# Taking the second block of the first group into the V product unnormalised, and normalising both blocks afterwards

## The chip, the cores and the metric

One core of one Trainium2 chip. The metric is the device time of one execution in microseconds (us). TensorE multiplies matrices and writes its results to PSUM; VectorE and ScalarE do the elementwise work; GpSimd stores most results to HBM and takes reciprocal square roots; SyncE issues the loads.

## The reference, cut to what matters

One encoder layer on x of 2048 positions by 1024 channels:

```python
h = rms_norm(x, norm_g[l])                      # x * rsqrt(mean(x*x)) * g, by position
proj = jnp.einsum("bsd,de->bse", h, w_in[l])    # 6 parts of 1024 columns
a_val, a_gate, g_conv, u, v, g_sgu = jnp.split(proj, split_points, axis=-1)
y_conv = conformer_conv_branch(a_val, a_gate, ...) * silu(g_conv)
y_sgu = (u * (w_s @ layer_norm(v) + b_s)) * silu(g_sgu)   # w_s: 128x128 by head, in chunks of 128 positions
x = x + jnp.einsum("bse,ed->bsd", jnp.concatenate([y_conv, y_sgu], -1), w_out[l])
return rms_norm(x, final_g)
```

The change concerns the first lines: how h is formed for the first 1024 positions, and when it has to exist for the part called v. Because the factor rsqrt(mean(x*x)) belongs to a position, it can be multiplied into h before the product or into a row of v after it.

## The kernel before, in words

Every fp32 operand is split into a high part in fp32r and the remainder (`split`, L127: ScalarE makes the high part, VectorE the low part), and each product is three matrix products: high by high, low by high, high by low. The positions stand in four blocks of 512. A group is two blocks: group 0 is blocks 0 and 1, group 1 is blocks 2 and 3. `group(g, A, vtiles)` runs once for each.

A group begins with V, the 1024 columns of v in two halves. `v_mm(A, b, half, tiles, done, hooks)` (L192) multiplies one block by one half of the columns: 96 matmuls of 128x512, over 8 k-steps, 3 products and 4 chunks of 128 positions, into 4 PSUM tiles. A hook is a call written behind k-step k. So V is four such calls: blocks 0 and 1 with the first half, then both with the second half. `done` takes the four PSUM tiles out: for the first half to `v0t` and on to HBM, for the second half into `z`, whose mean and variance are taken, normalised (L288, ScalarE) and passed chunk by chunk to `mix` (L213): 8 small matmuls into two `mixp` tiles, copied by ScalarE to `mixt` (L220) and stored.

Behind V come 20 units. A unit is seven products of 12 matmuls each (a scheme with seven in place of eight block products), named x, z, y, v and again x and v by their PSUM tiles (L347). The operands are sums of blocks of a (s1 to s4, `sums_of_a`) and of weights (`unit_weights`, L304), whose raw tiles `w` are loaded by SyncE at L311 and L312 into the small pool of three row tiles. The same pool holds the first three chunks' `z`, the raw V weights `vraw` and, ahead of group 1, the raw `xs` of blocks 2 and 3. A depthwise convolution (L464 to L478) fills VectorE at low priority. Towards the end of group 0 the same stream of code makes group 1's h (`staged_h`: VectorE L143, then split into `a`) and splits group 1's V weights (`v_weights`: `vh` on ScalarE, `vl` on VectorE). Group 1's V begins when these are there.

At the very start of group 0, block 0 doesn't wait for its mean square. `X[0]` is x scaled by g alone, split into high and low (`xg`, L544 and L545), and `v0_done_scaled` (L251) multiplies each chunk's rows by the factor `row_rs[0]` as it takes them out of PSUM. Block 1 in before is normalised first: `squares` (L550) gives sums of squares, `stats_of` a factor by position (matmuls `pc`, VectorE `col`, GpSimd `rs`), `rows_of` spreads it over partitions (VectorE `dg`, matmul `rb_x`), and `normalise` multiplies and splits x (VectorE L143, then `a` on ScalarE and VectorE).

The program is written in this order, but a scheduler of the framework decides at build time in which order each engine gets its instructions, by priorities and by a timeline that it simulates; on the chip each engine's order is fixed.

## Time and profile before

| what | us |
|---|---|
| median of 3 runs | 1380.39 (1379.97 to 1381.41) |
| the profiled execution's own time | 1378.5 |
| its span in the trace | 1376.7 |
| TensorE busy in it | 1342.3 |
| VectorE busy in it | 1134.8 |
| ScalarE busy in it | 584.8 |

The span is the profiled execution's first to last instruction; 1.8 us of that execution's own time lie around it, and the median of the runs is another 1.9 us above it. A busy share near the whole span says that an engine had work nearly always, not that each of its instructions ran at its best rate.

### The profile page before, as it was taken

To read this page: it belongs to the slowest core of one execution; us is meant where nothing else is said; L and a number is where in the kernel's file an instruction comes from. 1 tells how busy PE (TensorE), PEld (TensorE's weight loads), DVE (VectorE), ACT (ScalarE), POOL (GpSimd) and SP (SyncE) were. 2 spreads that over 40 slices of the span, in tenths; PEclk is the share of its full clock that TensorE was granted. 3 is DMA by queue.
4 is the path that set the end of the run, shared out by engine and by line. 5 is a ranking of instruction groups with operands and counts; after the bars stand their busy time and mean duration, and the time that the engine had idled before them with its cause. 6 is when DMAs were issued, how large, how long until landed. Compare 5 with 4: busy or idle time off the path is not lost.

```text
span 1376.7 us, 17691 instructions
## 1 busy us (share of the span) xinstructions
PE 1342.3 (97%) x6044; PEld 1108.7 (81%) x6044; DVE 1134.8 (82%) x1787; ACT 584.8 (42%) x987; POOL 198.0 (14%) x378
## 2 busy tenths in 40 slices
PE   7999999999999999999999999999999999999996
PEld 5688888888888878878888888888878888888875
DVE  6975599999899999999899999998998224677763
ACT  5547444443545443353322222221344333656652
POOL 0101323323323310110111011110000000010110
PEclk9999999999999999999999999999999999999998
DMA  6227999898989885369877778777689444555541
GB/s 249 85 88 250 372 345 324 302 315 298 320 300 343 292 301 191 98 236 337 291 252 262 254 261 293 261 262 258 211 262 296 163 152 163 158 175 180 171 147 46
DMA packets 167450, 329.14 MB, mean 239 GB/s; under 512 B 15040, under 2 KB 84672, under 8 KB 167360
## 3 DMA queue, kind: packets, MB, share of 16 engines
q1 hardware_dynamic: 119040, 208.46, 45.9%
q0 software_dynamic: 31424, 111.17, 22.3%
q10 hardware_dynamic: 16896, 8.39, 2.2%
q8 instruction: 47, 0.77, 0.2%
q14 instruction: 43, 0.35, 0.1%
HBM read 191.12 MB, written 136.84 MB: 238 GB/s over the span
## 4 chain that ended last, share of the span: by engine, by line
PE 73%; DVE 11%; issue 9%; DMA 4%; POOL 1%; ACT 1%; SPq 0%; POOLq 0%; DVEq 0%; ACTq 0%
PE x L347 17%; PE pa L703 13%; PE po L703 12%; PE v L347 11%; PE v L198 7%; PE y L347 6%; PE z L347 5%; DVE ca L469 2%; DVE cb L477 2%; PE mixp L218 1%; DVE cb L471 1%; DMA xrow<-in_x_dram 1%; DVE op L130 1%; DMA mix_sp<-mixt 1%; DMA op_sp<-ex 1%
## 5 line engine op out<-in xcount | busy, mean ns | idle before, releaser
L469 DVE SCALAR_TENSOR_TENSOR ca<-cx,cwt,ca 128x505 f32<-128x505 f32 (+1 forms) x240 | 180.5, 752 | 0.0
L471 DVE SCALAR_TENSOR_TENSOR cb<-cx,cwt,cb 128x504 f32<-128x504 f32 (+1 forms) x224 | 168.2, 751 | 6.7 <-ACT cb L465 2.8
L477 DVE SCALAR_TENSOR_TENSOR cb<-cq,cws,cb 128x504 f32<-128x504 f32 (+1 forms) x224 | 167.6, 748 | 0.5
L347 PE MATMUL x<-s,op 128*128 128x512 f32 x624 | 151.6, 390 | 1.4 <-ACT s L129 1.4
L347 PEld LDWEIGHTS x<-s,op 128*128 128x128 f32 x624 | 116.8, 188 | 26.2 <-ACT s L129 1.7
L198 PE MATMUL v<-vh,a 128*128 128x512 f32 x448 | 121.0, 394 | 3.7 <-ACT a L129 3.4
L198 PEld LDWEIGHTS v<-vh,a 128*128 128x128 f32 x448 | 84.2, 189 | 23.2 <-ACT a L129 4.2
L347 PE MATMUL z<-s,op 128*128 128x512 f32 x336 | 82.2, 391 | 0.7 <-DVE s L130 0.5
L347 PE MATMUL x<-s,ex 128*128 128x512 f32 x336 | 81.4, 390 | 0.0
L347 PE MATMUL x<-a,op 128*128 128x512 f32 x312 | 79.1, 391 | 0.0
L347 PE MATMUL y<-a,op 128*128 128x512 f32 x312 | 76.1, 391 | 0.8 <-DMA op<-op_sp 0.8
L347 PE MATMUL v<-s,op 128*128 128x512 f32 x312 | 75.3, 390 | 0.0
L347 PE MATMUL v<-a,op 128*128 128x512 f32 x312 | 75.1, 390 | 0.1
L347 PEld LDWEIGHTS z<-s,op 128*128 128x128 f32 x336 | 62.7, 188 | 14.2 <-DVE s L130 0.9
L347 PEld LDWEIGHTS x<-s,ex 128*128 128x128 f32 x336 | 62.9, 188 | 12.9
L130 DVE TENSOR_TENSOR op<-w,op 128x512 fp32r<-128x512 f32 x92 | 62.2, 690 | 9.6 <-ACT op L129 9.6
L198 PE MATMUL v<-vl,a 128*128 128x512 f32 x224 | 68.5, 394 | 1.0 <-DVE vl L130 1.0
L347 PEld LDWEIGHTS y<-a,op 128*128 128x128 f32 x312 | 58.4, 188 | 13.7 <-DMA op<-op_sp 1.2
L418 ACT ACTIVATE y<-x 128x512 f32<-128x512 f32 x40 | 23.3, 582 | 108.3 <-PE x L347 108.3
L347 PEld LDWEIGHTS v<-a,op 128*128 128x128 f32 x312 | 58.5, 188 | 12.7 <-DVE t L434 0.5
L347 PEld LDWEIGHTS x<-a,op 128*128 128x128 f32 x312 | 58.5, 188 | 12.5 <-issue 0.5
L320 POOL DMA_DIRECT2D op_sp<-op x92 | 49.2, 535 | 132.1 <-DVE op L130 122.3
(165 smaller groups left out, 2693.3 us busy)
## 6 DMA issues: line engine op xcount, KB each, us to landing
op_sp<-op POOLq DMA_DIRECT2D x92, 512.0 KB, 5.9
op<-op_sp SPq DMA_DIRECT2D x92, 512.0 KB, 4.6
op_sp<-ex POOLq DMA_DIRECT2D x48, 512.0 KB, 6.1
ex<-op_sp SPq DMA_DIRECT2D x48, 512.0 KB, 4.4
w<-in_w_dram SPq DMA_DIRECT2D x40, 512.0 KB, 6.8
vraw<-in_w_dram SPq DMA_DIRECT2D x32, 256.0 KB, 4.9
mix_sp<-mixt ACTq DMA_DIRECT2D x32, 256.0 KB, 6.2
glu_sp<-sig POOLq DMA_DIRECT2D x64, 128.0 KB, 4.8
```

What stands on the lines that cost most here:

```text
L130: nc.vector.tensor_tensor(lo, src, hi.bitcast(F32), op=sub)
L198: nc.tensor.matmul(pss[c], A[b, k // 4][:, apart, k % 4, c * P:(c + 1) * P], tiles[k // 2][wpart][:, :, k % 2, :], start=k == 0 and p == 0 ...
L218: nc.tensor.matmul(px[:, h * P:(h + 1) * P], zc[half][:, h * P:(h + 1) * P], wsv[half][:, h * P:(h + 1) * P], start=True, stop=True)
L320: nc.gpsimd.dma_start(op_sp[n * 7 + j], t)
L347: nc.tensor.matmul(acc, tv[:, wpart, kk, :], a[:, apart, kk, :], start=start and p == 0 and kk == 0, stop=p == 2 and kk == 3, skip_group_c ...
L418: nc.scalar.activation(y, x0, AF.Copy)
L469: stt(a, e[:, j:j + M + 1], cwt[:, i, 2 * j:2 * j + 1], a, mul, add)
L471: stt(b, o[:, j:j + M], cwt[:, i, 2 * j + 1:2 * j + 2], b, mul, add)
L477: stt(b, q[:, j:j + M], cws[:, i, j:j + 1], b, mul, add)
L703: nc.tensor.matmul(po[h], lw[:, b % 2 * 4 + k, :], rh[:, k, h * SG:(h + 1) * SG], start=False, stop=stop and p == 2 and k == 3, skip_group ...
```

## The change

A second unnormalised operand `X[1]` (`xh`) is built from block 1 as `X[0]` is from block 0: eight more ScalarE instructions and eight more on VectorE. Block 1's first half of V reads it, and its four chunks are scaled by their rows' factors on the way out. The squares of block 0 are written ahead of those of block 1. The statistics of block 0 are hooked to the end of block 0's product, its spread and all of block 1's to block 1's product, and both blocks are normalised after the two products; only the second half of V and the units read the normalised `a`.

```diff
         def v0_done_scaled(c, pv):
             t = ttile("v0t")
-            nc.scalar.activation(t, pv, AF.Identity, scale=row_rs[0][:, c:c + 1])
+            nc.scalar.activation(t, pv, AF.Identity, scale=row_rs[c // 4][:, c % 4:c % 4 + 1])
             nc.vector.bn_stats(stats[:, c, 0, :], t)
             nc.gpsimd.dma_start(v_sp[c], t)
...
     for i in range(4):
         piece(1, i)
+    for k in range(NK):
+        if k % 4 == 0:
+            X[1, k // 4] = btile([P, 2, 4, SG], F32R, f"xh{k // 4}")
+        hi, lo = X[1, k // 4][:, 0, k % 4, :], X[1, k // 4][:, 1, k % 4, :]
+        nc.scalar.activation(hi, part_of(1, k), AF.Copy, scale=norm_g[:, k:k + 1])
+        nc.vector.scalar_tensor_tensor(lo, part_of(1, k), norm_g[:, k:k + 1], hi.bitcast(F32), mul, sub)
...
+    squares(0)
     squares(1)
-    squares(0)
...
         if g == 0:
-            def both():
-                rows_of(1)
-                rows_of(0)
-
-            v_mm(X, 0, 0, vtiles, v0_done_scaled, {3: lambda: stats_of(1), 4: lambda: stats_of(0), 5: both})
+            v_mm(X, 0, 0, vtiles, v0_done_scaled, {5: lambda: stats_of(0)})
+            v_mm(X, 1, 0, vtiles, v0_done_scaled, {1: lambda: rows_of(0), 3: lambda: stats_of(1), 5: lambda: rows_of(1)})
+            normalise(0)
             normalise(1)
-            normalise(0)
         else:
             v_mm(A, 0, 0, vtiles, v0_done)
-        v_mm(A, 1, 0, vtiles, v0_done)
+            v_mm(A, 1, 0, vtiles, v0_done)
```

The scheduler's orders change at three places that matter below.

**The start of ScalarE.** Here `x_110` is block 0's x, `xg` its scaled high part, `vh` the high part of a piece of V's weights. Before:

```order
L544 ACTIVATE xg_112<-x_110,vec 128x512 x2
L129 ACTIVATE vh<-vraw 128x1024
L544 ACTIVATE xg_112<-x_110,vec 128x512 x2
L129 ACTIVATE vh<-vraw 128x1024
L544 ACTIVATE xg_113<-x_110,vec 128x512 x2
L129 ACTIVATE vh<-vraw 128x1024
L544 ACTIVATE xg_113<-x_110,vec 128x512 x2
L129 ACTIVATE vh<-vraw 128x1024
```

With the change:

```order
L544 ACTIVATE xg_112<-x_110,vec 128x512 x2
L560 ACTIVATE ss<-x_110 128x512
L560 ACTIVATE sq<-x_110 128x512
L129 ACTIVATE vh<-vraw 128x1024
L544 ACTIVATE xg_112<-x_110,vec 128x512 x2
L560 ACTIVATE sq<-x_110 128x512 x2
L129 ACTIVATE vh<-vraw 128x1024
L544 ACTIVATE xg_113<-x_110,vec 128x512 x2
```

The two first squares of block 0 (L560, in before L554) now stand ahead of the first `vh`, which the first matmul reads, and further pairs of squares stand between the later ones.

**The first unit, on TensorE.** The last `v` matmuls of V's second half, then the unit's products; `mixp` x8 is one chunk's mix. Before, the first chunk's mix stands 37 `v` matmuls ahead of these rows:

```order
L198 MATMUL v_796<-vl,a_0_378 128x512
L198 MATMUL v_796<-vh,a_0_378 128x512
L347 MATMUL x_1028<-a_0_391,op_0_987 128x512 x2
L218 MATMUL mixp<-wsv,z 128x128 x8
L347 MATMUL x_1028<-a_0_391,op_0_987 128x512 x10
L218 MATMUL mixp<-wsv,z 128x128 x8
L347 MATMUL z<-s_0_570,op_1_995 128x512 x12
L218 MATMUL mixp<-wsv,z 128x128 x8
L347 MATMUL x_1028<-s_0_571,op_2_1000 128x512 x4
L347 MATMUL y<-a_0_404,op_3_1006 128x512 x4
```

With the change the first chunk's mix stands here, inside the last k-step of the last block:

```order
L198 MATMUL v_814<-vh,a_0_538 128x512
L198 MATMUL v_811<-vh,a_0_538 128x512
L218 MATMUL mixp<-wsv,z 128x128 x8
L198 MATMUL v_811<-vl,a_0_538 128x512
L198 MATMUL v_811<-vh,a_0_538 128x512
```

and 11 `v` matmuls behind it the unit begins:

```order
L198 MATMUL v_814<-vl,a_0_538 128x512
L198 MATMUL v_814<-vh,a_0_538 128x512
L347 MATMUL x_1046<-a_0_499,op_0_1005 128x512 x12
L347 MATMUL z<-s_0_588,op_1_1013 128x512 x12
L218 MATMUL mixp<-wsv,z 128x128 x20
L347 MATMUL x_1046<-s_0_589,op_2_1018 128x512 x4
L347 MATMUL y<-a_0_512,op_3_1024 128x512 x4
L347 MATMUL x_1046<-s_0_589,op_2_1018 128x512 x8
L218 MATMUL mixp<-wsv,z 128x128 x8
L347 MATMUL y<-a_0_512,op_3_1024 128x512 x8
```

The first mix stands 26 matmuls nearer to the unit, and of the others two and a half (`x20`) now stand in a row behind z, where before they lay one by one between the products. On ScalarE the copies of these mixes stand so with the change (`z<-z,mv` is the normalising of the last four chunks, L288; `y<-x` reads the finished first product):

```order
L129 ACTIVATE s_0_589<-r_791 128x512
L220 ACTIVATE mixt<-mixp 128x512
L418 ACTIVATE y<-x_1046 128x512
L221 DMA mix_sp<-mixt 128x4x128
L220 ACTIVATE mixt<-mixp 128x512
L288 ACTIVATE z<-z,mv 128x1024 x3
L129 ACTIVATE s_0_591<-r_793 128x512
L288 ACTIVATE z<-z,mv 128x1024
L221 DMA mix_sp<-mixt 128x4x128
L220 ACTIVATE mixt<-mixp 128x512 x2
L129 ACTIVATE ex<-w_1_1007 128x512
L221 DMA mix_sp<-mixt 128x4x128 x2
```

Before, the same place reads:

```order
L273 ACTIVATE z<-v_795 128x512
L273 ACTIVATE z<-v_796 128x512
L220 ACTIVATE mixt<-mixp 128x512
L221 DMA mix_sp<-mixt 128x4x128
L220 ACTIVATE mixt<-mixp 128x512
L221 DMA mix_sp<-mixt 128x4x128
L288 ACTIVATE z<-z,mv 128x1024 x4
L418 ACTIVATE y<-x_1028 128x512
L220 ACTIVATE mixt<-mixp 128x512
L129 ACTIVATE ex<-w_1_989 128x512
```

Behind the normalising there stand now the copies of the second mix's halves; before it was those of the third.

**VectorE ahead of group 1.** `a_1_...` are low parts of group 1's h, `xs` its raw tiles, `vl` the low parts of group 1's V weights, `t` and `z` sums of the last unit's products, `m` and `sgs` that unit's results. Before, up to the first `vl` of group 1:

```order
L130 TENSOR_TENSOR a_1_4324<-xs,a_1_4324 128x512
L473 TENSOR_TENSOR cx<-ca,cb 128x504
L130 TENSOR_TENSOR a_1_4341<-xs,a_1_4341 128x512
L434 TENSOR_TENSOR t_4475<-v,z_4371 128x512
L130 TENSOR_TENSOR a_1_4341<-xs,a_1_4341 128x512
L389 TENSOR_TENSOR m<-sgs,m 128x512
L143 SCALAR_TENSOR_TENSOR xs<-xs,vec,rb_x 128x512 x2
L474 SCALAR_TENSOR_TENSOR cb<-ca,vec,cb 128x504
L387 SCALAR_TENSOR_TENSOR m<-m,vec,ad 128x512
L437 TENSOR_TENSOR z_4371<-x_4287,z_4371 128x512
L130 TENSOR_TENSOR vl<-vraw,vh 128x1024
```

With the change:

```order
L130 TENSOR_TENSOR a_1_4359<-xs,a_1_4359 128x512
L437 TENSOR_TENSOR z_4389<-x_4305,z_4389 128x512
L130 TENSOR_TENSOR a_1_4359<-xs,a_1_4359 128x512
L387 SCALAR_TENSOR_TENSOR m<-m,vec,ad 128x512
L130 TENSOR_TENSOR a_1_4359<-xs,a_1_4359 128x512
L474 SCALAR_TENSOR_TENSOR cb<-ca,vec,cb 128x504
L130 TENSOR_TENSOR a_1_4359<-xs,a_1_4359 128x512
L388 SCALAR_TENSOR_TENSOR sgs<-t_4493,sgs 128x512
L388 SCALAR_TENSOR_TENSOR sgs<-z_4389,sgs 128x512
L387 SCALAR_TENSOR_TENSOR m<-m,vec,ad 128x512
L475 SCALAR_TENSOR_TENSOR cb<-cq,cws,cb 128x504
L130 TENSOR_TENSOR vl<-vraw,vh 128x1024
```

All four low parts of the second `a` tile now stand ahead of the first `vl`, where two stood before, and with them both `sgs`, a further `m` and a convolution step (L475). Counted from the first sum of the last unit's weights that reads both raw tiles (`w<-w,w`, L323), the first `vl` is the 45th instruction behind it before and the 53rd with the change; the last read of the `xs` tile whose room the first `vraw` takes (`a<-xs`, the first row before) is the 34th and the 41st.

## Rows read from the trace of the kernel before

**Rows 1.** The page, busy time by engine (share of the span), instructions.

```profile
PE 1342.3 (97%) x6044; PEld 1108.7 (81%) x6044; DVE 1134.8 (82%) x1787; ACT 584.8 (42%) x987; POOL 198.0 (14%) x378
```

**Rows 2.** TensorE's waits by releaser: us in total, times, longest.

```profile
PE v L198 <- ACT vh L129: 10.0, 2, 9.6
```

**Rows 3.** Windows: busy us of each engine (instructions), clock, DMA.

```profile
40.00:50.00 10.00, 10.00 (x31) 7.07 (x32) 10.00 (x20) 4.46 (x8) 0.20 (x1) 0.76 0.21 78
```

**Rows 4.** Timeline of TensorE, 34 to 46 us: start, duration, what, [idle before].

```profile
34.55 0.95 PE L124 MATMUL pc<-ones,ss 128*128 128x1 f32 x8
35.36 1.10 PE L118 MATMUL rb_x<-dg,ones 128*128 128x512 f32 x2
39.82 2.08 PE L198 MATMUL v<-vh,a 128*128 128x512 f32 x4 [3.36 <-ACT a L129]
...
45.67 2.13 PE L198 MATMUL v<-vh,a 128*128 128x512 f32 x8
```

**Rows 5.** Timeline of ScalarE, first 23 us.

```profile
6.72 1.33 ACT L544 ACTIVATE xg<-x,vec 128x512 fp32r<-128x512 f32 x2
8.53 1.06 ACT L129 ACTIVATE vh<-vraw 128x1024 fp32r<-128x1024 f32 x1 [0.47 <-DMA vraw<-in_w_dram]
...
22.95 3.74 ACT L554 ACTIVATE sq<-x 128x512 f32<-128x512 f32 x7
```

**Rows 6.** Timeline of TensorE around the first unit.

```profile
101.82 1.95 PE L218 MATMUL mixp<-wsv,z 128*128 128x128 f32 x16
...
112.01 0.62 PE L347 MATMUL x<-a,op 128*128 128x512 f32 x2
...
122.27 2.15 PE L218 MATMUL mixp<-wsv,z 128*128 128x128 f32 x16 [1.06 <-ACT mixt L220]
124.31 1.19 PE L347 MATMUL x<-s,op 128*128 128x512 f32 x4
```

**Rows 7.** Timeline of ScalarE around the first unit.

```profile
107.37 0.63 ACT L129 ACTIVATE op<-w 128x512 fp32r<-128x512 f32 x1 [0.22 <-DMA w<-in_w_dram]
...
116.58 4.64 ACT L288 ACTIVATE z<-z,mv 128x1024 f32<-128x1024 f32 x4 [1.31 <-DVE mv L284]
```

**Rows 8.** Timeline of SyncE's queue, the first unit's weights.

```profile
103.85 0.33 SPq L311 DMA_DIRECT2D w<-in_w_dram  x1
114.48 0.33 SPq L312 DMA_DIRECT2D w<-in_w_dram  x1
```

**Rows 9.** Timeline of VectorE around the first unit.

```profile
109.48 0.69 DVE L130 TENSOR_TENSOR s<-r,s 128x512 fp32r<-128x512 f32 x1
110.08 0.69 DVE L323 TENSOR_TENSOR w<-w 128x512 f32<-128x512 f32 x1
...
119.19 1.29 DVE L323 TENSOR_TENSOR w<-w,w 128x512 f32<-128x512 f32 x2 [2.65 <-DMA w<-in_w_dram]
```

**Rows 10.** Timeline of TensorE where group 1 begins.

```profile
503.77 2.88 PE L347 MATMUL x<-s,ex 128*128 128x512 f32 x12
506.49 3.00 PE L347 MATMUL v<-a,ex 128*128 128x512 f32 x12
509.82 1.19 PE L198 MATMUL v<-vh,a 128*128 128x512 f32 x4 [0.33 <-ACT vh L129]
512.05 1.20 PE L198 MATMUL v<-vl,a 128*128 128x512 f32 x4 [1.03 <-DVE vl L130]
```

**Rows 11.** Timeline of VectorE ahead of group 1.

```profile
482.36 0.69 DVE L323 TENSOR_TENSOR w<-w,w 128x512 f32<-128x512 f32 x1 [1.58 <-DMA w<-in_w_dram]
...
503.94 0.69 DVE L130 TENSOR_TENSOR a<-xs,a 128x512 fp32r<-128x512 f32 x1
...
510.77 1.23 DVE L130 TENSOR_TENSOR vl<-vraw,vh 128x1024 fp32r<-128x1024 f32 x1
```

**Rows 12.** Timeline of ScalarE ahead of group 1.

```profile
508.71 1.06 ACT L129 ACTIVATE vh<-vraw 128x1024 fp32r<-128x1024 f32 x1 [5.28 <-DMA vraw<-in_w_dram]
```

**Rows 13.** Timeline of SyncE's queue ahead of group 1.

```profile
504.65 3.20 SPq L187 DMA_DIRECT2D vraw<-in_w_dram  x4
```

## The prediction

> **What bounds the kernel now.** I read the busy times first: TensorE is busy for 97% of the span [rows 1]. No engine can be unloaded to gain much; what can be gained is the few places where TensorE stands or runs below its rate. So I read its waits next. The largest is 9.6 us on the first `vh`, the start, of which the change removes nothing [rows 2]. The change aims at a smaller hole, behind block 0's product, so I read that stretch as a timeline and by windows. Then I walked along the new orders with the durations of before, from the start to where they come out in step again, because a scheduler has set the whole of group 0 anew.
>
> The rate first: 12 matmuls from 503.77 to 506.49 [rows 10], that is 2.72 us or 0.227 each.
>
> **The hole that is removed.** Block 0's product is done at 34.55. Then come the second sums `pc` and the two `rb_x`, a wait of 3.36 for block 1's `a`, and four matmuls that take from 39.82 on about twice their time (2.08 for four, where the rate gives 1.2 with the drain of the last) [rows 4]. The granted clock explains that: 0.76 over 40 to 50 us, with 31 matmuls [rows 3], so TensorE spent about half of this window at 1.2 GHz in place of 2.4. At 45.67 the rate is nearly back. These 11.12 us hold `pc` 0.81 (34.55 to 35.36), three pairs like `rb_x` (one, the other, and the row sums `rsum`) of some 0.85 each, estimated from the 1.10 of a pair [rows 4] less the drain, and 8 matmuls of V, 1.81. Together 5.2, so 5.9 us are lost. With the change block 1's matmuls stand right behind block 0's and read `xh`, so nothing is waited for, and the clock should not fall. The bounds of this gain: 3.4, if the clock falls all the same, and 5.9. I take 5.9, since a stretch without a wait in front has no reason in these rows to slow down.
>
> **What it adds, hidden.** Eight `xh` on ScalarE at 0.67 (two `xg` take 1.33 [rows 5]) are 5.3 us; ScalarE's squares were done at 26.7 (22.95 and 3.74 [rows 5]), so with them it is done by 32.0. TensorE reads the first `xh` at 35 and the last k-step 19 us later. VectorE's eight low parts, 0.6 to 0.7 each by its pitch of 0.60 [rows 9], follow two by two. The cover is block 0's product and most of block 1's, about 40 us of TensorE. Without it the price would be up to 5.3. The normalising is moved behind: 16 multiplications and 16 low parts, some 20 us of VectorE at that pitch, of which block 0's half is needed when block 1's product ends, near 57, after a spread hooked to its second k-step, near 41, and block 1's another 21.8 later. Both fit. Block 1's four statistics now read `v0t` in SBUF in place of PSUM, and its four stores leave from ScalarE's scaled copy as block 0's did: no instruction more, cost nothing.
>
> **What it moves at the start.** Two squares stand ahead of the first `vh`. That `vh` began at 8.53 after an idle 0.47, so ScalarE was free at 8.06. Two squares at 0.53 (7 in 3.74) end at 9.12 [rows 5]: TensorE starts 0.6 later. Bounds 0 and 0.7. Later pairs are hidden, since each piece of weights lasts TensorE for 24 matmuls, 5.4 us, against 3.5 of ScalarE. So TensorE leads by 5.9 - 0.6 = 5.3 through V, and the last block ends at 112.01 - 5.3 = 106.7 [rows 6].
>
> **What it loses at the first unit.** Four waits arise in that order, each from something that doesn't come earlier by as much:
> 1. The unit's first weights are loaded into the row tile that chunk 0's mix sets free: that mix began at 101.82 [rows 6], and SyncE issued at 103.85 [rows 8]. They landed and were split from 107.37 [rows 7], 3.52 later, and TensorE needed them at 112.01, 4 us of slack. Now the mix stands 11 matmuls ahead of the unit and ends at 106.7 - 2.5 = 104.2. So the split ends at 104.2 + 3.5 + 0.63 = 108.35: 1.65 lost.
> 2. x lasts 2.72, to 111.05. The low part of the second operand stands on VectorE behind six full instructions and four tiny ones, counted from the first's landing: 108.35 + 6 x 0.60 + 0.4 + 0.7 = 113.05 [rows 9]. z uses it from its fifth matmul, 111.95: 1.1 lost. z ends at 114.85, the second mix at 116.55.
> 3. The third mix needs a `mixt` copied, and ScalarE has that behind the normalising of the last chunks, four z of 4.64 in all [rows 7] and one split of 0.6, which begin when VectorE has the means, about 113.85 by the walk of point 2. So the copy ends at 113.85 + 5.2 + 0.6 = 119.65: 3.1 lost. Before, this wait was 1.06 [rows 6].
> 4. The unit's second weights take the row tile of the second mix: issued at 116.55 in place of 114.48 [rows 8], with the 4.7 that they took before (VectorE waited for them until 119.19 [rows 9]) at 121.25. Two `ex` on ScalarE wait for them and for a sum of them, to 123.1, then the next `mixt`, to 123.7. The third mix was done at 121.35: 2.35 lost.
>
> Then half a mix, and the third product begins at 124.5, against 124.31 before [rows 6], with half a mix (0.86) less done. So TensorE is 1.05 late where it led by 5.3. Bounds: points 1 and 2 follow from queue orders alone, but 3 and 4 fall away if loads land at once and VectorE comes earlier, which leaves a lead of 3; if the second load takes 3 us longer it is 4 late.
>
> Whether such waits bring the clock down too is not in these terms. The row for it is the window behind the wait of 3.36, with 0.76 [rows 3, 4]; no row shows waits of 1 to 3 us in a row. I leave the price out, and it is a rival below. The Trainium skill's page "TensorE: Matmul & The Clock Gate" (What's actually happening) says that the clock falls to half after idle time and comes back under sustained work; by that page it could fall here as well, and TensorE would be some 3.4 late in place of 1.05. The trace agrees with it at the hole above, and at the first unit of before it shows nothing on it.
>
> **What it loses where group 1 begins.** TensorE had group 1's first matmuls at 509.82 after 0.33 of waiting for `vh` and the next four at 512.05 after 1.03 for `vl` [rows 10]. Neither has slack, so any delay on VectorE is TensorE's. VectorE is without a gap from the sum of the last unit's weights at 482.36, held up by a DMA, to `vl` at 510.77 [rows 11]: 45 instructions in 28.41, 0.631 each. With the change there are 53: eight more, 5.05 us. The other route: `vraw` was issued at 504.65 [rows 13], when the `a` begun at 503.94 had read its `xs` [rows 11]; `vh` began at 508.71, released by that DMA [rows 12]. With 41 in place of 34 instructions the issue comes 7 x 0.635 = 4.4 later. The later route counts, 5.05. It is counted from a DMA's landing ahead of the last unit, and takes up the 1.05 from above: a TensorE that comes 1.05 late waits that much less. If the load moves with TensorE, both add to 6.1. If VectorE reaches that place up to 5 us earlier, because the filler was moved, nothing is left of it: bounds 0 and 6.1. I take 5.05, since this stretch is held by instructions that stand in a fixed order.
>
> **The sum.** In the profiled execution: 1378.5 + 5.05 = 1383.5. The median of the runs is 1.9 above that execution, so the forecast is 1380.4 + 5.05 = **1385.4**. Its terms: -5.9 hole, +0.6 start, +6.35 first unit (8.2 of waits, less the 1.06 and some 0.7 of smaller waits that stood there: 112.01 to 124.31 hold 10.6 of work at the rate), +4.0 at group 1.
>
> **The rivals.** About 0.2%, 2.8 us, is what a measurement can tell here: faster is below 1377.6, slower above 1383.2.
> - The lead is kept to the end (faster): the loads land early and the copies come in time, and VectorE's fillers shift so that `vl` comes with the lead. For it: ScalarE is idle over half the time [rows 1]. Against it: points 1 and 2 are orders. 1380.4 - 5.3 = 1375.1. It decides from the point where TensorE begins the third product before 122 and group 1 before 507.
> - Only the first unit takes the lead, and group 1's `vl` is in step (no change): 1380.4 + 1.05 = 1381.4. For it: eight instructions are few of the 700 or so that VectorE has behind it by then, and its filler can be early as well as late.
> - The clock falls in the first unit too: four waits of 1 to 3 us follow each other within 17 us, and one of 3.36 brought 1.2 GHz before [rows 3, 4]. At half rate for the ten matmuls behind that would cost 10 x 0.227 = 2.3, 1383.7 with group 1 in step; where `vl` sets the end it is swallowed there. Against it: work lies between the waits.
> - Everything adds: the last load moves with TensorE, 6.1, and the weights of the second load take 2 us longer: 1388.5.
> - That the change doesn't do what it says I hold for excluded: the new order has block 1's matmuls right behind block 0's.
>
> **How the numbers follow.** Forecast (1383.3 to 1387.0) 0.44; first unit alone 0.22; the lead kept 0.17; all adds 0.10; clock in the first unit 0.07, half of it each side of the bound. Faster 0.17; same 0.22 + 0.03 = 0.25; slower 0.44 + 0.10 + 0.04 = 0.58. The range goes down to the lead kept, 1375.0 (half of that case lies below), and up to 1388.5 (half of the last above): 0.13 left out.
>
> **What would show it.** In the changed profile: TensorE without a wait from its start to the end of V, clock 1.00 in 40 to 50, the last block done near 106.7. Then waits of x on a DMA or on `op`, of z on `op`, of `mixp` on `mixt` twice, and the third product near 124.5. Group 1's first `vl` near 516 and TensorE's wait for it 4 to 5 us. I am wrong if the mixes run without waits (step 3 or 4 at the first unit), or if `vl` of group 1 comes at 511 or earlier: then the counted instructions weren't what set its time.

## The result, and the profile after

| what | before | after |
|---|---|---|
| median of 5 runs each, us | 1381.41 (1379.97 to 1384.88) | 1397.05 (1392.80 to 1399.96) |
| ratio | | 1.0122 [1.0105, 1.0139] |
| the profiled execution, us | 1378.5 | 1392.8 |
| its span, us | 1376.7 | 1391.0 |

The change makes the kernel 1.2% slower. The forecast was 1385.4 with a range up to 1388.5: the direction is right, the time lies above the range.

The page's busy line shows at once that no engine got noticeably more work; TensorE's 4.6 us more at the same number of matmuls are matmuls at a lower rate [rows 1].

```profile
PE 1346.9 (97%) x6044; PEld 1112.9 (80%) x6044; DVE 1138.8 (82%) x1795; ACT 589.5 (42%) x995; POOL 202.9 (15%) x378
```

Its largest waits of TensorE (us in total, times, longest); in before only the start [rows 2] and the hole's 3.4 were of this size:

```profile
PE v L198 <- ACT vh L129: 15.4, 2, 10.0
PE mixp L218 <- ACT mixt L220: 3.6, 2, 2.1
PE v L347 <- DVE t L434: 3.0, 1, 3.0
...
PE x L347 <- ACT op L129: 1.9, 1, 1.9
PE x L347 <- DVE op L130: 1.1, 1, 1.1
```

The first row holds the start's 10.0 and a new wait of 5.4; the others that are new lie at the first unit and in group 1.

Windows (the seventh figure, behind POOL's, is the granted clock):

```profile
40.00:50.00 10.00, 10.00 (x48) 8.01 (x47) 8.60 (x13) 6.62 (x10) 0.00 (x0) 1.00 0.17 53
110.00:120.00 10.00, 9.21 (x36) 7.53 (x36) 6.59 (x17) 7.71 (x11) 4.36 (x3) 0.68 0.48 157
120.00:130.00 10.00, 6.46 (x29) 5.78 (x30) 5.17 (x8) 6.34 (x11) 2.13 (x4) 0.66 0.72 219
520.00:530.00 10.00, 9.47 (x30) 7.17 (x31) 10.00 (x14) 3.85 (x4) 1.08 (x2) 0.70 0.80 258
```

The hole of [rows 3] is gone: 48 matmuls in place of 31 between 40 and 50 us, at full clock. But the clock now falls at three other places. TensorE's timeline shows them in turn:

```profile
34.45 0.39 PE L198 MATMUL v<-vh,xg 128*128 128x512 f32 x1
34.67 0.62 PE L198 MATMUL v<-vh,xh 128*128 128x512 f32 x2
...
106.11 0.39 PE L198 MATMUL v<-vh,a 128*128 128x512 f32 x1
108.42 1.20 PE L347 MATMUL x<-a,op 128*128 128x512 f32 x4 [1.93 <-ACT op L129]
110.77 3.78 PE L347 MATMUL x<-a,op 128*128 128x512 f32 x8 [1.14 <-DVE op L130]
114.35 3.85 PE L347 MATMUL z<-s,op 128*128 128x512 f32 x12
118.04 1.95 PE L218 MATMUL mixp<-wsv,z 128*128 128x128 f32 x16
122.05 2.79 PE L218 MATMUL mixp<-wsv,z 128*128 128x128 f32 x16 [2.07 <-ACT mixt L220]
126.33 2.08 PE L218 MATMUL mixp<-wsv,z 128*128 128x128 f32 x8 [1.49 <-ACT mixt L220]
128.06 2.05 PE L347 MATMUL x<-s,op 128*128 128x512 f32 x4
...
509.07 2.88 PE L347 MATMUL x<-s,ex 128*128 128x512 f32 x12
...
520.03 2.07 PE L198 MATMUL v<-vh,a 128*128 128x512 f32 x4 [5.36 <-ACT vh L129]
522.61 2.07 PE L198 MATMUL v<-vl,a 128*128 128x512 f32 x4 [0.51 <-DVE vl L130]
...
745.88 2.33 PE L347 MATMUL v<-a,ex 128*128 128x512 f32 x9 [2.96 <-DVE t L434]
```

Block 1's `xh` follows block 0's `xg` without a gap, and V's last matmul begins at 106.11. Eight x behind the second wait take 3.78 where the rate gives 1.8, and four at 128.06 and at 520.03 take 2.05 and 2.07 where 1.2 is usual: half rate.

A ledger of the two profiled executions, each at the same amount of TensorE's work done (counted in matmuls, small ones by their share, so that a moved mix doesn't matter):

| stretch | lost (+) or gained | late after it |
|---|---|---|
| start | +0.35 | +0.35 |
| to the end of V | -6.0 | -5.7 |
| first unit | +11.2 | +5.5 |
| where group 1 begins (503 to 543) | +6.5 | +12.05 |
| 605 to 650 | -1.75 | +10.3 |
| wait for `t` near 742 | +3.25 | +13.55 |
| rest | +0.7 | +14.3 |

The end is the difference of the spans. The medians lie 15.6 apart; the 1.3 beyond the profiled pair I have no trace for. The runs of after spread over 7 us, and the profiled one is the fastest of them.

The other engines at the first unit. SyncE's queue, the first and the second half of the unit's weights [rows 8]:

```profile
104.06 0.33 SPq L311 DMA_DIRECT2D w<-in_w_dram  x1
120.05 0.33 SPq L312 DMA_DIRECT2D w<-in_w_dram  x1
```

The timeline of ScalarE [rows 7]:

```profile
107.74 0.63 ACT L129 ACTIVATE op<-w 128x512 fp32r<-128x512 f32 x1 [0.61 <-DMA w<-in_w_dram]
...
116.35 1.25 ACT L288 ACTIVATE z<-z,mv 128x1024 f32<-128x1024 f32 x1
...
121.42 1.06 ACT L220 ACTIVATE mixt<-mixp 128x512 f32<-128x512 f32 x2
```

GpSimd's reciprocal square root for the last chunks, in before and then in after:

```profile
115.30 1.04 POOL L99 TENSOR_TENSOR mv<-mv,vec 128x4 f32<-128x4 f32 x1 [2.25 <-DVE mv L282]
```

```profile
112.91 3.21 POOL L99 TENSOR_TENSOR mv<-mv,vec 128x4 f32<-128x4 f32 x1 [1.31 <-DVE mv L282]
```

And VectorE's timeline, of the second block's normalising, and ahead of group 1 [rows 11]:

```profile
56.00 0.87 DVE L105 TENSOR_SCALAR dg<-ident,rs 128x128 f32<-128x128 f32 x4 [0.94 <-POOL rs L99]
...
62.59 4.04 DVE L143 SCALAR_TENSOR_TENSOR x<-x,vec,rb_x 128x512 f32<-128x512 f32 x6
...
116.15 0.17 DVE L284 SCALAR_TENSOR_TENSOR mv<-mv 128x4 f32<-128x4 f32 x1 [0.93 <-POOL mv L99]
...
487.82 0.69 DVE L323 TENSOR_TENSOR w<-w,w 128x512 f32<-128x512 f32 x1 [2.26 <-DMA w<-in_w_dram]
...
521.34 1.21 DVE L130 TENSOR_TENSOR vl<-vraw,vh 128x1024 fp32r<-128x1024 f32 x1
```

Two things are to be seen. The normalising of the last chunks begins at 116.35, and in before at 116.58 [rows 7], though TensorE had V done 5.7 us earlier. More than one engine has a share in that. VectorE had its part of the means (L282) done at 112.82, 2.4 us earlier than in before; GpSimd's root behind it then took 3.21 in place of 1.04. ScalarE was busy until 116.28 with splits and copies in its own order, one of which had waited 3.05 for a sum of VectorE (L171). And from 487.82 to 521.34 are 33.52 us for the 53 instructions counted in the prediction, 0.632 each; but the start of the count has itself moved from 482.36 [rows 11] to 487.82, 5.46 later, just as TensorE had.

### The profile page after: what moved, and what is told of

It is laid out like the page before. It is cut to its first block, busy times and chain, and to the rows that moved or that the text cites. A ratio compares the mean times of both kernels' runs of the same rounds, so it can differ in the third digit from the quotient of the medians.

```text
span 1391.0 us, 17698 instructions
## 1 busy us (share of the span) xinstructions
PE 1346.9 (97%) x6044; PEld 1112.9 (80%) x6044; DVE 1138.8 (82%) x1795; ACT 589.5 (42%) x995; POOL 202.9 (15%) x378
## 4 chain that ended last, share of the span: by engine, by line
PE 80%; DVE 10%; DMA 5%; issue 2%; ACT 2%; POOL 0%; SPq 0%; DVEq 0%; POOLq 0%; ACTq 0%
PE x L347 20%; PE v L347 13%; PE pa L706 12%; PE po L706 11%; PE v L198 8%; PE z L347 6%; PE y L347 6%; PE mixp L218 2%; DVE ca L469 1%; DVE cb L477 1%; DMA m<-mix_sp 1%; DVE cb L471 1%; DVE s L130 1%; DMA w<-in_w_dram 1%; DVE r L170 1%
## 5 line engine op out<-in xcount | busy, mean ns | idle before, releaser
L198 PE MATMUL v<-vh,a 128*128 128x512 f32 x384 | 105.5, 397 | 5.4 <-ACT vh L129 5.4
L198 PEld LDWEIGHTS v<-vh,a 128*128 128x128 f32 x384 | 73.2, 191 | 21.9 <-ACT vh L129 5.8
L347 PE MATMUL v<-s,op 128*128 128x512 f32 x312 | 75.3, 390 | 0.0
L130 DVE TENSOR_TENSOR op<-w,op 128x512 fp32r<-128x512 f32 x92 | 61.0, 682 | 13.4 <-ACT op L129 13.4
L129 ACT ACTIVATE op<-w 128x512 fp32r<-128x512 f32 x92 | 54.4, 624 | 40.6 <-DVE w L323 29.4
```

The source lines that it names most:

```text
L129: nc.scalar.activation(hi, src, AF.Copy)
L130: nc.vector.tensor_tensor(lo, src, hi.bitcast(F32), op=sub)
L198: nc.tensor.matmul(pss[c], A[b, k // 4][:, apart, k % 4, c * P:(c + 1) * P], tiles[k // 2][wpart][:, :, k % 2, :], start=k == 0 and p == 0 ...
L347: nc.tensor.matmul(acc, tv[:, wpart, kk, :], a[:, apart, kk, :], start=start and p == 0 and kk == 0, stop=p == 2 and kk == 3, skip_group_c ...
```

## The experiments

Two theories of the first unit are set against each other, which the expectations call T and V. **T**: the loss comes from where the mixes stand, since they free the row tiles that the weights are loaded into. **V**: it comes from VectorE, which normalises block 1 later than before (its multiplications begin at 62.59 in place of 36.50; in before it was block 0's that came last, at 49.74) and carries that on through the sums of a, the means and the low parts to the first unit, so that TensorE's lead meets nothing that is ready. Most of the edits below let the scheduler place the mixes anew as well, so that few runs change the one without the other. For group 1 the theory is the count: VectorE's fixed order puts so many instructions ahead of `vl`. "Late" is against before, at equal work. Of each experiment one execution is profiled. The 8 matmuls of a mix are 16 records in the trace.

**Weights earlier, mixes moved.** The addend is made behind the first unit, the first mixes are written ahead of it and the unit's first matmul is held behind them. The edit also drops two early weight builds of group 1's first unit, so of this run only group 0 is read.

```diff
-        v_mm(A, 0, 1, t1, v1_done, {2: make_addend(wsv)} if g == 0 else None)
+        v_mm(A, 0, 1, t1, v1_done)
...
+        if g == 0:
+            hooks = {1: hooks[1], 3: hooks[3]}
         v_mm(A, 1, 1, t1, v1_done, hooks)
+        if g == 0:
+            mix_next()
...
                 if n == 0:
                     mix_next()
+                if g == 0 and n == 0 and j in (2, 3):
+                    mix_next()
                     if j < 4:
                         build()
                 build()
+                if g == 0 and n == 1 and j == 1:
+                    make_addend(wsv)()
```

> Edit: the addend (its eight small VectorE instructions and two tiles) moves from the middle of V behind the first unit, and the first two mixes stand ahead of the unit on TensorE. Theory T (the first unit is late because its weights wait for row tiles that the mixes set free, and the waits bring TensorE's clock down): the waits at the first unit shrink below 1 us, the clock stays at 1.00 from 100 to 140 us, and TensorE, 5.5 late there with the change, is 4 to 5.7 ahead of the kernel before; group 1's first vl stays the 53rd instruction behind its anchor, so the loss there stays: about 10 less than with the change, 1386 to 1388. Rival R (VectorE's sixteen more instructions and the normalising behind the products make everything late, whatever stands where on TensorE): under 4 gained, 1393 or more.

Measured: 1404.54 (1401.40 to 1408.73), ratio 1.0171 [1.0140, 1.0202]. On TensorE the unit begins with a mix:

```profile
111.78 3.78 PE L218 MATMUL mixp<-wsv,z 128*128 128x128 f32 x16 [7.18 <-ACT mixt L220]
```

On ScalarE that copy stands behind splits that wait for VectorE's sums:

```profile
108.52 0.63 ACT L129 ACTIVATE s<-r 128x512 fp32r<-128x512 f32 x1 [2.96 <-DVE r L171]
...
111.15 1.07 ACT L220 ACTIVATE mixt<-mixp 128x512 f32<-128x512 f32 x2
```

The weights were in time, x waited for none, and TensorE lost 7.18 us all the same, on a copy that stands in ScalarE's queue behind VectorE. The time lies in rival R's range. T alone is not the cause.

**The addend alone behind the first unit.**

```diff
-        v_mm(A, 0, 1, t1, v1_done, {2: make_addend(wsv)} if g == 0 else None)
+        v_mm(A, 0, 1, t1, v1_done)
...
                 build()
+                if g == 0 and n == 1 and j == 1:
+                    make_addend(wsv)()
```

> Edit: the addend alone moves behind the first unit. The first mix then stands 37 matmuls ahead of the unit, as in the kernel before, two and a half mixes in a row behind z as with the change, and group 1's first vl is the 45th instruction behind its anchor, as before. Theory T: no wait of x on op; mixt and the second weights are still waited for, 2 to 4 us in all with the clock down or not; at group 1 no more than 2 lost: 1383 to 1388. Rival R: as for the edit with the mixes, 1393 or more.

Measured: 1400.33 (1398.67 to 1401.95), 1.0139 [1.0116, 1.0162]. The two waits of x are gone, a wait of 3.9 for `mixt` with a lower clock behind it stands in their place; the first unit loses 7.7 in place of 11.2. (In after, a sum on VectorE had waited 2.61 for the store of the addend, until 96.46; that wait is gone here as well.) The time lies in rival R's range. `vl` of group 1 is the 45th as in before, and still 8.4 us are lost there, behind waits of 4.23 for `vh` and 1.74 for `vl`: a miss. VectorE there:

```profile
497.37 0.69 DVE L323 TENSOR_TENSOR w<-w,w 128x512 f32<-128x512 f32 x1
...
525.61 1.21 DVE L130 TENSOR_TENSOR vl<-vraw,vh 128x1024 fp32r<-128x1024 f32 x1
```

From the first sum to `vl` are 28.24, as the count has it. But that sum, the count's anchor, comes 15.01 later than in before while TensorE is 8.8 late, and VectorE does not wait for a load there: it is still busy with other work. So the place in the count is not all that sets the crossing; where the count begins is the rest.

**The first piece of V weights ahead of the third block's h.**

```diff
                     if g == 0 and n == NU - 1:
+                        gv = v_weights(0)
+                        nv = next(gv)
                         staged_h(nextA, 2, rb[2])
...
-                    nv = None
-                    for nv in v_weights(0):
+                    for nv in gv:
                         pass
```

> Edit: the first piece of group 1's V weights is loaded and split ahead of the raw h tiles; the first vl is then the 13th instruction behind its anchor, the second the 54th. Theory T: group 1's start is late by VectorE's order and the row tile behind it: TensorE's wait there falls from 5.4 to about 2 and the clock stays up, so 4 to 6 less than with the change, 1391 to 1393; the first unit as it was. Rival: the wait is one on transfers or on h itself, and stays: 1396 to 1398.

Measured: 1391.22 (1387.88 to 1395.21), 1.0070 [1.0044, 1.0096]. Up to the crossing it runs as after does, 5.4 late. The first piece's `vl` comes in time, but TensorE then waits 2.80 for a second `vh` and 1.81 for its `vl`, at a lower rate behind, and is 12.7 late at 543 where after was 12.05. The profiled run then has no wait of 3 for `t` and ends 13.5 late, after 14.3. The median lies in T's range, but it is lower by more than the profile explains: inconclusive for the crossing, beyond that one piece earlier doesn't free it, since the next stands where it stood.

**TensorE kept busy in the first wait.** 14 matmuls are added, whose result the first product overwrites.

```diff
         x0 = ptile("x0")
+        if g == 0 and filler[0]:
+            filler[0] = False
+            for _ in range(14):
+                mm = nc.tensor.matmul(x0, a11[:, 0, 0, 0:P], a11[:, 0, 0, :], start=True, stop=True, skip_group_check=True)
+                tc.keep_in_program_order(mm)
         product(x0, a11, ring.pop(0), True)
```

> Edit: 14 more matmuls of 128x512, whose result is overwritten, stand between V and the first unit's first product, 3.2 us at full rate, where TensorE waited 1.9 and 1.1. Theory T: the clock stays at 1.00 from 100 to 120, x and z run at full rate, the second mix ends about 3 earlier, and the third product 2 to 4 earlier: 1392 to 1395 if nothing else moves. Rival (the waits alone cost, the clock nothing): 1397 or slightly more, since the extra matmuls last a little longer than the waits.

Measured: 1392.93 (1391.22 to 1393.41), 1.0083 [1.0061, 1.0104]. The windows of the first unit:

```profile
110.00:120.00 10.00, 8.69 (x43) 6.38 (x41) 7.42 (x18) 6.89 (x10) 2.59 (x3) 1.00 0.46 152
120.00:130.00 10.00, 7.22 (x28) 6.49 (x29) 5.69 (x9) 7.20 (x12) 2.66 (x5) 0.66 0.71 215
```

TensorE's timeline there:

```profile
107.25 3.34 PE L419 MATMUL x<-a 128*128 128x512 f32 x14
110.42 1.07 PE L347 MATMUL x<-a,op 128*128 128x512 f32 x4
111.69 2.11 PE L347 MATMUL x<-a,op 128*128 128x512 f32 x8 [0.20 <-DVE op L130]
...
122.78 3.78 PE L218 MATMUL mixp<-wsv,z 128*128 128x128 f32 x16 [3.29 <-ACT mixt L220]
126.21 2.05 PE L347 MATMUL x<-s,op 128*128 128x512 f32 x4
```

The clock holds at 1.00 between 110 and 120, where after had 0.68, and the eight x take 2.11 in place of 3.78. So there it was the waits that brought it down. But the time gained there is mostly waited away: `mixt` is as late as in after (the wait is 3.29 in place of 2.07), the third product begins 1.85 earlier, and at the second unit, the 14 matmuls left out of the work, this run is 6.1 late and after 5.5. The first unit loses 10.9 here and 11.2 in after. The clock is real, but holding it up in this stretch doesn't shorten the unit, because the copies come no earlier. Behind their wait it falls here too (0.66), so what it costs there is not taken away. The time lies in T's range, though not for T's reason: from the second unit to 543 only 2.1 are lost (`vl` is the 50th), and a wait of 5.5 for `s` near 610 takes most of that back, so that the span is 1.6 below that of after.

**Less and more in front of VectorE.** In the next three runs, and in the two under "Where the statistics may stand", the code of the units is untouched; the order that the scheduler gives them is not. First the statistics of block 1 at the end of block 0's product:

```diff
-            v_mm(X, 0, 0, vtiles, v0_done_scaled, {5: lambda: stats_of(0)})
-            v_mm(X, 1, 0, vtiles, v0_done_scaled, {1: lambda: rows_of(0), 3: lambda: stats_of(1), 5: lambda: rows_of(1)})
+            v_mm(X, 0, 0, vtiles, v0_done_scaled, {5: lambda: stats_of(0), 6: lambda: stats_of(1)})
+            v_mm(X, 1, 0, vtiles, v0_done_scaled, {1: lambda: rows_of(0), 2: lambda: rows_of(1)})
```

> Edit: the sums and factors of block 1 are hooked one k-step behind those of block 0, still in block 0's product, and its spread one k-step behind block 0's. Block 1's normalising can then start about 10 us earlier. Theory V (VectorE stands still behind block 0 and carries that time as a lateness to the sums of a, the splits and the means at the first unit): the first unit loses 4 to 7 in place of 11.2; group 1's vl is the 50th instruction, 3 to 5 lost there: 1388 to 1393. Theory T (row tiles and mixes alone): the first mix stands 18 matmuls ahead of the unit in place of 11, so only the first wait goes and the first unit loses about 9: 1394 to 1397.

Measured: 1383.18 (1382.19 to 1385.84, 9 runs), 1.0023 [1.0010, 1.0036]. 14 us of the 16 lost are back by an edit that removes and adds no instruction. The time is below both ranges, and little of it is won at the first unit: that loses 9.2, which T had right and V (4 to 7) had not. The two profiled executions differ by 9.7. Of these 2.0 come from the first unit and 1.0 from the crossing; the rest lies behind 543, where among others the wait for `t` near 742 is missing.

The other way, the low parts of `xh` computed twice (eight more instructions on VectorE, ahead of the normalising):

```diff
         nc.vector.scalar_tensor_tensor(lo, part_of(1, k), norm_g[:, k:k + 1], hi.bitcast(F32), mul, sub)
+        nc.vector.scalar_tensor_tensor(lo, part_of(1, k), norm_g[:, k:k + 1], hi.bitcast(F32), mul, sub)
```

> Edit: the eight low parts of xh are computed twice, 8 more VectorE instructions of 0.6 to 0.7 us (5.4 us) ahead of the normalising; nothing else in the source. Group 1's first vl is the 45th instruction behind its anchor, as in the kernel before. Theory V (VectorE's work in V bounds the first unit): the first unit loses 14 to 17. Theory T: still 10 to 12, since VectorE stands still there anyway. Both: at group 1 0 to 2 lost in place of 6.5, so 1394 to 1398 by V and 1390 to 1393 by T.

Measured: 1385.75 (1383.81 to 1388.02), 1.0049 [1.0032, 1.0065]. The first unit loses 14.8, more than after, as V has it. But the scheduler has moved the first mix too: it stands 1 matmul ahead of the unit in place of 11, so T's mechanism could do it as well. And yet the kernel is faster than after, and below both ranges, because nothing (0.1) is lost where group 1 begins and the wait for `t` near 742 is missing. VectorE where group 1 begins:

```profile
492.01 0.69 DVE L323 TENSOR_TENSOR w<-w,w 128x512 f32<-128x512 f32 x1 [1.72 <-DMA w<-in_w_dram]
...
520.41 1.21 DVE L130 TENSOR_TENSOR vl<-vraw,vh 128x1024 fp32r<-128x1024 f32 x1
```

`vl` is the 45th instruction again, and comes 28.40 behind the anchor; in before it was 28.41 [rows 11]. The anchor is 9.65 later, as late as TensorE is (9.6). That is the count shown without the lateness in it: here the order decides the crossing's loss, and the lateness goes through unchanged.

The order of the squares as in before, all else as after:

```diff
-    squares(0)
     squares(1)
+    squares(0)
```

> Edit: the squares of block 1 are written ahead of those of block 0 again, as in the kernel before; the rest of the change stays. TensorE starts 0.3 to 0.6 earlier. Both spreads now come later on TensorE (its 56th and 138th matmul behind block 0 in place of the 27th and 110th), so VectorE stands still longer: by theory V the first unit loses as much or more than with the change, 11 to 15, and group 1's first vl, the 49th, 2 to 4: 1393 to 1400. Rival (the order of the squares is what costs, by the start and ScalarE's queue): 1388 or less.

Measured: 1399.75 (1397.70 to 1402.78), 1.0149 [1.0133, 1.0166]. The last multiplication of the normalising begins at 75.3 in place of 67.2, and the first unit loses 18.2. The time is as V had it; the first unit loses more than the 11 to 15, and the crossing 7.0 in place of 2 to 4. The first mix stands right ahead of the unit here.

**The crossing with its filler taken away.** The convolution's loops run over 4 taps each, so that 12 of its 43 tap instructions remain (the convolution is then not the reference's); once on before, once on after:

```diff
-        for j in range(1, 16):
+        for j in range(1, 5):
             stt(a, e[:, j:j + M + 1], cwt[:, i, 2 * j:2 * j + 1], a, mul, add)
-        for j in range(1, 15):
+        for j in range(1, 5):
             stt(b, o[:, j:j + M], cwt[:, i, 2 * j + 1:2 * j + 2], b, mul, add)
...
-        for j in range(1, 15):
+        for j in range(1, 5):
             stt(b, q[:, j:j + M], cws[:, i, j:j + 1], b, mul, add)
```

> The kernel before with 12 of the 43 tap instructions of each convolution left in (the output is not the convolution's): VectorE has two thirds of its work, and 41 instructions stand between the anchor and group 1's first vl. It takes VectorE's filler away from both kernels, so that only their difference counts. Expected 1370 to 1380, the start and the first unit as in the kernel before.

> The changed kernel with the same taps left out; its order at the first unit is that of the changed kernel, and from the last unit on that of few_taps_before. If the loss at group 1 is VectorE's filler in a fixed order: 5 to 7 above few_taps_before, all of it from the first unit (11 lost, 5.7 won before). If it comes from transfers or tiles: 12 to 15 above.

Measured: 1380.21 (1378.43 to 1384.78), 1.0005 [0.9991, 1.0018], and 1384.76 (1383.65 to 1391.82), 1.0053 [1.0029, 1.0077], both against before. `vl` is the 41st in both. VectorE on the way there in the first and in the second:

```profile
475.42 1.29 DVE L323 TENSOR_TENSOR w<-w,w 128x512 f32<-128x512 f32 x2 [3.04 <-DMA w<-in_w_dram]
...
506.35 1.22 DVE L130 TENSOR_TENSOR vl<-vraw,vh 128x1024 fp32r<-128x1024 f32 x1
```

```profile
481.12 1.29 DVE L323 TENSOR_TENSOR w<-w,w 128x512 f32<-128x512 f32 x2 [2.85 <-DMA w<-in_w_dram]
...
512.58 1.22 DVE L130 TENSOR_TENSOR vl<-vraw,vh 128x1024 fp32r<-128x1024 f32 x1
```

With one order in both kernels, group 1 begins without a loss in either (each gains some 2 us on before there), while the first unit of the second still loses 9.6. So the change's loss at the crossing comes from VectorE's filler, and the first unit's does not. VectorE isn't bound by the count in these two: it waits for loads of `xs` on the way (4.67 and 4.49 at the longest). The medians lie 4.6 apart, a little under the 5 to 7. With a good part of VectorE's work gone the first kernel is no faster than before (the top of its range was 1380): between 400 and 440 the two lose 3.2 and 5.9 on before, which no run explains.

**Where the statistics may stand.** Two more places of the hooks. One step earlier throughout:

```diff
-            v_mm(X, 0, 0, vtiles, v0_done_scaled, {5: lambda: stats_of(0)})
-            v_mm(X, 1, 0, vtiles, v0_done_scaled, {1: lambda: rows_of(0), 3: lambda: stats_of(1), 5: lambda: rows_of(1)})
+            v_mm(X, 0, 0, vtiles, v0_done_scaled, {4: lambda: stats_of(0), 5: lambda: stats_of(1)})
+            v_mm(X, 1, 0, vtiles, v0_done_scaled, {0: lambda: rows_of(0), 1: lambda: rows_of(1)})
```

> Edit: as in the run with the earlier statistics, but each hook one k-step earlier (2.7 us). The mixes now stand singly between the parts of x and z; group 1's first vl is the 50th instruction. Theory V: the first unit loses 4 to 7, group 1 4 to 5.5: 1380 to 1384. Rival S: 1383 to 1388.

Measured: 1385.93 (1383.30 to 1387.98), 1.0046 [1.0029, 1.0063]. The first unit proper loses 3.3, another 5.2 follows before the second unit begins, and the crossing takes 7.3 with `vl` the 50th: more than the 4 to 5.5 that the count gave. Both are misses for V (4 to 7 at the first unit), and the time lies in rival S's range, above V's.

And with block 0's spread still in block 0's product:

```diff
+            v_mm(X, 0, 0, vtiles, v0_done_scaled, {4: lambda: stats_of(0), 5: lambda: stats_of(1), 6: lambda: rows_of(0)})
+            v_mm(X, 1, 0, vtiles, v0_done_scaled, {0: lambda: rows_of(1)})
```

> Edit: both blocks' sums and the spread of block 0 are hooked to block 0's product (k-steps 4, 5 and 6), block 1's spread to the first k-step of block 1's product: some 3 us ahead of the run with the earlier statistics. Theory V (the first unit is late by the time that VectorE stands still behind block 0; group 1 by the instructions in its fixed order): the first unit loses 3 to 6 of the 5.5 won, in place of 9; the first vl of group 1 is the 45th instruction, as in the kernel before, and 0 to 2 are lost there: 1376 to 1381, at or under the kernel before. Rival S (VectorE's eight more instructions cost what they last, wherever they stand): 1383 to 1388, as in the run with the earlier statistics.

Measured: **1377.12** (1373.57 to 1381.93, 12 runs), 0.9980 [0.9966, 0.9994]: faster than both kernels, by 3.1 us than before's 1380.24 in the same runs and by 20 than the change as made. VectorE, then TensorE:

```profile
53.28 5.36 DVE L143 SCALAR_TENSOR_TENSOR x<-x,vec,rb_x 128x512 f32<-128x512 f32 x8
```

```profile
107.19 1.19 PE L347 MATMUL x<-a,op 128*128 128x512 f32 x4 [0.92 <-ACT op L129]
109.17 3.68 PE L218 MATMUL mixp<-wsv,z 128*128 128x128 f32 x16 [0.78 <-ACT mixt L220]
112.60 2.09 PE L347 MATMUL x<-a,op 128*128 128x512 f32 x8
...
120.77 1.17 PE L347 MATMUL x<-s,op 128*128 128x512 f32 x4
```

ScalarE, the normalising of the last chunks:

```profile
119.47 4.63 ACT L288 ACTIVATE z<-z,mv 128x1024 f32<-128x1024 f32 x4
```

The time lies in V's range, and rival S (1383 to 1388) is out. The second normalising of h begins at 53.28, 9.3 earlier than in after and 3.5 later than in before. The first unit's waits are 0.92 and 0.78, mixes lie between the parts of x, and the third product begins at 120.77 against 128.06. Of the lead of 6.0 that V gives, 3.3 are left behind the first unit and 3.2 at the end. The statistics inside block 0's product cost TensorE no wait. The last chunks' normalising comes no earlier by it: it begins 3.1 later than in after, and no longer matters, since the copies of the first mixes stand ahead of it on ScalarE. So part of what is won is order.

The versions side by side:

| version | last multiplication of the normalising begins | matmuls from the first mix to the unit, in the trace | lost from the end of V to the second unit | place of `vl` |
|---|---|---|---|---|
| before | 54.4 | 37 | 0 | 45 |
| stats_in_block0 | 57.9 | 15 | 2.6 | 45 |
| stats_step_earlier | 57.1 | 16 | 8.6 | 50 |
| stats_early | 56.3 | 17 | 9.2 | 50 |
| after | 67.2 | 11 | 11.2 | 53 |
| low_parts_twice | 70.2 | 1 | 14.8 | 45 |
| squares_as_before | 75.3 | 0 | 18.2 | 49 |
| addend_behind | 68.8 | 37 | 7.7 | 45 |

The later VectorE has h, the more is lost at the first unit. It is no law of one number: three versions near 57 differ by 6.6, and the place of the first mix orders the versions almost as well. Only the run with the addend behind sets the two apart: with the mix as far ahead as in before and h as late as in after, 7.7 are lost. So the mix's place alone is not the cause. How much of the rest is VectorE's lateness, and how much the order that the scheduler makes of it, these runs don't separate.

The crossing can be followed further in the same traces. In each of these versions `vl` comes 0.63 us per counted instruction behind the anchor; what differs is how late the anchor is, which need not be how late TensorE is:

| version | anchor late | TensorE late | from the anchor to `vl` (before: 28.41) | anchor beyond TensorE, plus count | lost at the crossing |
|---|---|---|---|---|---|
| low_parts_twice | 9.65 | 9.5 | 28.40 | 0.1 | 0.1 |
| busy_in_wait | 5.26 | 6.8 | 31.40 | 1.4 | 1.4 |
| stats_in_block0 | -1.03 | -2.75 | 28.43 | 1.7 | 1.7 |
| stats_early | 6.00 | 3.8 | 31.52 | 5.3 | 5.3 |
| stats_step_earlier | 7.22 | 4.1 | 31.53 | 6.2 | 7.3 |
| after | 5.46 | 5.7 | 33.52 | 4.8 | 6.3 |
| squares_as_before | 16.29 | 13.4 | 30.83 | 5.3 | 7.0 |
| addend_behind | 15.01 | 8.8 | 28.24 | 6.0 | 8.4 |

(Here TensorE's lateness is taken at 470 and the loss from there to 543, hence 6.3 for after.) The last four lose 1.1 to 2.4 more than the sum, and in these four the granted clock falls furthest there (0.59 to 0.70 over ten us, against 0.83 or 1.00 in the others). In stats_early and stats_step_earlier TensorE's wait is named for `t`, which stands in the same order of VectorE.

## Why the prediction failed, point by point

**Right.** The hole closes: the step said -5.9 + 0.6, the runs show -5.7 at the end of V with the start 0.35 late; the clock stays at 1.00, and `xh` is hidden. At the first unit three of the four waits came true: x on `op` 1.93 (predicted 1.65), the third mix on `mixt` 2.07 (3.1), the last on `mixt` 1.49 (2.35). The fourth, 1.14, is another than the 1.1 of point 2: x's fifth matmul waited for the low part of the first operand, while the second operand's, which z was to wait for, was done at 114.62 and in time. That the sizes agree is luck. The eight instructions ahead of `vl` cost 33.52 - 28.41 = 5.11 (5.05).

**"What it adds, hidden", the words "Both fit".** This failed first. I asked whether the moved normalising is done before TensorE reads it, and it is: TensorE has no wait in V. I did not follow what stands behind it on VectorE. Block 1's spread waits for its statistics until 56.00, its multiplications begin at 62.59, and of what comes behind them ScalarE's normalising of the last chunks begins as late as in before, and the first low part later (110.07, in before 108.88). Moving the hooks alone shows that the place of this work is not free: 11.2 lost becomes 2.6 to 9.2, and the kernel 1377.12 at the best. I costed the move at nothing and named as its cover the work of TensorE. Link by link the way from the late normalising to the unit is not shown: between 90 and 103 VectorE stands for 5.9 us, 2.61 of them for the store of the addend and 2.68 for a split of ScalarE.

**"What it loses at the first unit", the term +6.35.** Measured 11.2. My walk had the means at 113.85 for point 3; VectorE's part was done at 112.82, but with GpSimd's 3.21 and ScalarE's own order the normalising began at 116.35, 2.5 later, and the `mixt` wait ended at 122.05 in place of 119.65. The second weights were issued at 120.05 in place of 116.55, because x and z ran at a lower rate: 20 matmuls from 110.77 to 118.04 are 7.27 us where the rate gives 4.5. That is the third rival's mechanism, which I gave a chance of 0.07 and a price of 2.3. Its direct price was 2.7 in x and z, 1.2 in the last mix (2.08 for 0.86) and some 0.8 in the four x behind; yet with the clock held up in the first of these stretches the unit lost 10.9 all the same. So the waits themselves were smaller than in the sum (6.6 for 8.2), and the half rate behind them, put at nothing, is where the rest of the 11.2 shows; but it can't be taken away by itself, since the copies that TensorE waits for come no earlier. The Trainium skill's page "TensorE: Matmul & The Clock Gate" (What's actually happening) has the clock fall after idle time; the trace agrees at 0.68 and 0.66, and leaving it out of the sum on the ground that work lies between the waits was wrong.

**"What it loses where group 1 begins", the words "takes up the 1.05".** I held the count's anchor to be fixed in time by a DMA, so that lateness and count would overlap. The load moves with TensorE, since the anchor came 5.46 later. `vl` then came 10.57 later than before [rows 11], 5.46 by lateness and 5.11 by count. This is the bound "if the load moves with TensorE, both add", which I had at 6.1 because I thought TensorE only 1.05 late. TensorE lost 6.5 there: 5.36 on `vh` and 0.51 on `vl`, where before had 1.36 of waits, and the lower clock behind them (0.70). The wait was named for `vl`; the trace names `vh` first.

**Not foreseen.** The wait of 2.96 for `t` near 742. VectorE's filler stands ahead of `t` there; that is argued from the order; the wait is missing in stats_early and low_parts_twice, but no run took it away by itself.

By the terms: -5.3 was -5.7; +6.35 was +11.2; +4.0 was +6.5; and 605 to the end, 0 in the forecast, was +2.2. Together 14.3 in place of 5.05.

**Open.** Why the anchor comes 2 to 6 us later than TensorE in four versions: in stats_early, stats_step_earlier and squares_as_before VectorE waits for the load there (5.64, 5.57 and 2.57), in addend_behind it is still busy. And what VectorE's lateness and the place of the mixes are each worth at the first unit.

## What to carry to other kernels

When work is moved off a bound engine's path, follow the engine it lands on to the next place where the two meet: here TensorE's lead of 5.7 us met operands and copies that were ready no earlier, and became a loss. Where each engine's order is fixed, count the instructions between a landing load and the one that is waited for, and ask whether that load moves with the delay; if it does, lateness and count add. Before giving up an idea that shows a closed hole and a slower kernel, try the same instructions hooked a step or two elsewhere: two lines of hooks were worth 20 us here, more than the idea.

## What was unexpected of the hardware

The clock can fall after quite short waits with work between them: to 0.68 over 110 to 120 us behind waits of 1.93 and 1.14, and in the fastest version 16 small matmuls still took 3.68 in place of 1.95 behind waits of 0.92 and 0.78 (0.87 granted over 110 to 120 us). It need not: in stats_step_earlier waits of 0.69 and 0.77 at the same two places left it at 1.00. And keeping TensorE busy with 14 matmuls that nobody reads (3.2 us) held it at 1.00, but bought almost nothing at that unit, because the copies that TensorE waited for next were no earlier.
